# Feed-forward of a hybrid encoder layer: two plain hidden blocks ahead of the seven-product ones

## The chip, the cores and the metric

One core of a Trainium2 chip runs the whole program. Its engines are TensorE (PE, matrix products; PEld is its weight load), VectorE (DVE), ScalarE (ACT), GpSimd (POOL) and SyncE (SP, which here issues the DMAs). The metric is the device time of one execution in microseconds (us). Executions of one kernel agree to some tenths of a per cent.

## The reference

One inference step of a conditioned layer over 512 prompt tokens and 8 x 16 sample tokens, 640 in all, with a model width of 1024. Two attention branches, their merge and a gated residual come first; the change is in what follows them, the feed-forward part:

```python
h = modulate(rmsnorm(x, g_norm_ffn), shift2, scale2)
return x + gate2 * ((jax.nn.silu(h @ w_gate) * (h @ w_up)) @ w_down)
```

`w_gate` and `w_up` are 1024 x 2816 and `w_down` is 2816 x 1024. All data are 32-bit floats.

## The kernel before, in words

**Precision.** Every matrix operand is split in a high and a low part (`split`, L84 to L88: a cast on ACT, L86, and a subtraction on DVE, L87). Each product is three matmuls, high by high, high by low and low by high (`mm3`, L92 to L96).

**Blocks.** The 2816 hidden columns are 22 blocks of 128 (`fb` from 0 to 21). A block needs `silu(h @ w_gate)` and `h @ w_up` for its 128 columns and all 640 tokens. The tokens are cut into two halves of 320 (64 of each tile of 128), the 1024 rows of `h` into two halves of 512 (four groups of 128).

**Plain block.** Block 0 is computed directly (`plain`, L1258): 8 row groups by three matmuls for gate and for up, first for tokens 0 to 383 (384 columns a matmul), then for 384 to 639 (256 columns). That fills four PSUM banks of the tag `mm`. `first_block` (L1309) then makes silu, product and split, and after that a combination of quarters of `h`, the "fourth sum": for two halves of it, three DVE operations into a tile `t4` (L1323 to L1325), then a split that writes it over quarter 1 of `hB`, the operand that holds `h` in quarters (`hB[0]` high, `hB[1]` low parts). `t4` has the tag `sums`, of which there is one buffer.

**Seven products.** Blocks 1 to 21 (`ff_block`, L1336) treat gate and up, row halves and token halves as a 2 by 2 by 2 scheme with seven products of 12 matmuls (320 columns each) where eight would do. In program order: a11 (with `hB` 0, in a bank `pa`), s1 (with `hS` 0, in `pb`), the former block's last product (a22, with `hB` 1, which holds the fourth sum), the new a11 (with `hS` 1), s4 (with `hB` 3), a12 (with `hB` 2, in `pc`) and a21 (with `hS` 2). s1 and s4 are made by POOL from the loaded weights (L1342, L1345, L1346) in a tile of the tag `sums`, the same buffer that `t4` uses. `pa` is a bank of tag `mm`, `pb` and `pc` of tag `tr`; each tag has four banks.

**Loads.** Weights come through four buffers `w_raw` (`load_raw`, L172 to L179), two to a block (gate and up). Split operands lie in 12 buffers `op_hi` and 11 `op_lo`. After block 1 the gate rows of the residual are made (`gate_rows`), which load one row tile through the same buffers. After blocks 5, 10, 14, 18 and the last one, `down` multiplies the hidden columns so far by `w_down`.

**What stands ahead.** The output projection ends with tokens 512 to 639; `h2_stats` and `h2_cols` turn each tile of 128 tokens into columns of `hB` and, on POOL, into the differences that become `hS`. PE runs the gate and up products of block 0 for tokens 0 to 383, the transposes of the last token tile (`h2_cols(4)`, L140), then block 0 for tokens 384 to 639. The three splits of `hS` follow on ACT and DVE.

**Order.** The program is traced in source order; a planner orders each engine's queue by a simulated timeline before the program runs, and gives out buffers of a tag as they come free. On the chip each engine runs its queue in that fixed order and waits on semaphores for data and for buffers.

Of the kernel before, what the change touches and what calls it, by code (L numbers as in the profile page):

```python
# [34 lines left out]
NFF = FF // P  # L35
# [13 lines left out]
def layer_kernel(  # L49
# [10 lines left out]
    def nm(s):  # L60
        uid[0] += 1
        return f"{s}_{uid[0]}"
# [12 lines left out]
    def mm_tile():  # L75
        return psum.tile([P, 512], F32, tag="mm", bufs=4, name=nm("mm"))

    def tr_tile():
        return psum.tile([P, 512], F32, tag="tr", bufs=4, name=nm("tr"))

    def f(ap):
        return ap.bitcast(F32)

    def split(hi, lo, src, scale=None, eng=None):  # L84
        if scale is None:
            S.copy(hi, src)  # L86
            (eng or V).tensor_tensor(out=lo, in0=src, in1=f(hi), op=ALU.subtract)  # L87
        else:  # L88
            S.activation(out=hi, in_=src, func=AF.Copy, scale=scale)
            (eng or V).scalar_tensor_tensor(out=lo, in0=src, scalar=scale, in1=f(hi), op0=ALU.mult, op1=ALU.subtract)  # L90

    def mm3(out, lh, ll, rh, rl, start, stop, more=False):  # L92

        T.matmul(out, lh, rh, start=start, stop=False, skip_group_check=more)  # L94
        T.matmul(out, lh, rl, start=False, stop=False, skip_group_check=more)  # L95
        T.matmul(out, ll, rh, start=False, stop=stop, skip_group_check=more)  # L96
# [988 lines left out]
    def operand(src, n=512):  # L1085
        hi = wa.tile([P, 512], F32R, tag="op_hi", bufs=12, name=nm("ophi"))[:, :n]
        lo = wa.tile([P, 512], F32R, tag="op_lo", bufs=11, name=nm("oplo"))[:, :n]
        split(hi, lo, src)
        return hi, lo
# [18 lines left out]
    def gate_rows(c0, scale):  # L1108

        raw = ada_rows(c0)  # L1110
        parts = []
        for c in range(2):
            hi = wa.tile([P, 512], F32R, tag="op_hi", bufs=12, name=nm("ophi"))[0:AR, :]
            lo = wa.tile([P, 512], F32R, tag="op_lo", bufs=11, name=nm("oplo"))[0:AR, :]
            split(hi, lo, raw[:, c * 512:(c + 1) * 512])
            parts.append((hi, lo))
        out = []
        for v in range(2):
            g_ = gp.tile([P, DM], F32, tag=f"gate{v}", name=nm("gate"))
            for c in range(2):  # L1120
                cc = slice(c * 512, (c + 1) * 512)
                ps = mm_tile()
                T.matmul(ps, selr[:, v * P:(v + 1) * P], parts[c][0], start=True, stop=False)
                T.matmul(ps, selr[:, v * P:(v + 1) * P], parts[c][1], start=False, stop=True)
                S.activation(out=g_[:, cc], in_=ps, func=AF.Copy, scale=scale)
            out.append(g_)
        return out
# [103 lines left out]
    def ff_raw(fb):  # L1231
        cs_ = slice(fb * P, (fb + 1) * P)
        return [load_raw(v[:, :, cs_], [KD, P])[0] for v in (wg_v, wu_v)]
# [21 lines left out]
    def operands_of(fb):  # L1255
        return [[operand(r[:, i:i + 512]) for i in (0, 512)] for r in ff_raw(fb)]

    def plain(bank, w, t0, t1):  # L1258
        for k in range(KD):
            ks = slice(k % 4 * P, (k % 4 + 1) * P)  # L1260
            h = [x[:, k // 4 * 2:k // 4 * 2 + 2, k % 4, t0 * 64:t1 * 64] for x in hB]
            mm3(bank[:, :(t1 - t0) * P].rearrange("p (a x) -> p a x", a=2), w[k // 4][0][:, ks], w[k // 4][1][:, ks],
                h[0], h[1], k == 0, k == KD - 1)

    w0 = operands_of(0)
    banks0 = [mm_tile() for _ in range(4)]
# [16 lines left out]
    with pool("fwork") as fw:  # L1283
# [19 lines left out]
        def new_hidden():  # L1303
            for h, tag in ((aT, "aT"), (aTl, "aTl")):
                h.append(fw.tile([P, NT], F32R, tag=tag, bufs=6, name=nm(tag)))

        aT, aTl, tail = [], [], []

        def first_block():  # L1309
            new_hidden()  # L1310
            for i, (t0, t1) in enumerate(((0, 3), (3, 5))):
                n = (t1 - t0) * P
                u = fw.tile([P, 512], F32, tag="tmp", bufs=2, name=nm("u"))[:, :n]
                S.activation(out=u, in_=banks0[2 * i][:, :n], func=AF.Silu)
                V.tensor_tensor(out=u, in0=banks0[2 * i + 1][:, :n], in1=u, op=ALU.mult)
                o = [h[-1].rearrange("p (t a x) -> p a t x", a=2, x=64)[:, :, t0:t1, :] for h in (aT, aTl)]
                split(o[0], o[1], u.rearrange("p (a t x) -> p a t x", a=2, x=64))

            for k in range(0, 4, 2):
                k2 = slice(k, k + 2)  # L1320
                t4 = fw.tile([P, 2 * 512], F32, tag="sums", name=nm("t4"))[:, :2 * HALF]
                t4 = t4.rearrange("p (k x) -> p k x", k=2)
                V.tensor_tensor(out=t4, in0=f(hB[0][:, 2, k2]), in1=f(hS[0][:, 1, k2]), op=ALU.subtract)  # L1323
                V.tensor_tensor(out=t4, in0=t4, in1=f(hB[1][:, 2, k2]), op=ALU.add)
                V.tensor_tensor(out=t4, in0=t4, in1=f(hS[1][:, 1, k2]), op=ALU.subtract)  # L1325
                split(hB[0][:, 1, k2], hB[1][:, 1, k2], t4)
# [9 lines left out]
        def ff_block(fb):  # L1336

            new_hidden()
            a11, a12, a21, a22 = quarters(fb)
            sums = fw.tile([P, 2, 512], F32, tag="sums", name=nm("sums"))  # L1340
            s1, s4 = sums[:, 0], sums[:, 1]
            G.tensor_tensor(out=s1, in0=a21, in1=a22, op=ALU.add)  # L1342
            V.tensor_tensor(out=a21, in0=a11, in1=a21, op=ALU.subtract)
            o11 = operand(a11)
            G.tensor_tensor(out=a11, in0=s1, in1=a11, op=ALU.subtract)  # L1345
            G.tensor_tensor(out=s4, in0=a12, in1=a11, op=ALU.subtract)  # L1346
            pa, pb, pc = mm_tile(), tr_tile(), tr_tile()
            product(pa, o11, hB, 0)
            u1 = part(pa, "u1", 2)
            product(pb, operand(s1), hS, 0)  # L1350
            u5 = part(pb, "u5")
            last_product()
            product(pa, operand(a11), hS, 1, start=False)
            u2 = part(pa, "u2")
            product(pb, operand(s4), hB, 3, start=False)
            V.tensor_tensor(out=u2, in0=pb[:, :HALF], in1=u2, op=ALU.add)
            S.activation(out=u2, in_=u2, func=AF.Silu)
            product(pc, operand(a12), hB, 2)
            V.tensor_tensor(out=u1, in0=pc[:, :HALF], in1=u1, op=ALU.add)
            S.activation(out=u1, in_=u1, func=AF.Silu)  # L1360
            product(pa, operand(a21), hS, 2, start=False)
            u3 = part(pa, "u3")
            G.tensor_tensor(out=u3, in0=u3, in1=u5, op=ALU.add)
            G.tensor_tensor(out=u2, in0=u2, in1=u3, op=ALU.mult)
            hidden(1, u2)
            tail.append((pa, u1, a22, [h[-1].rearrange("p (t a x) -> p t a x", a=2, x=64)[:, :, 0, :]
                                       for h in (aT, aTl)]))

        def down(f0, f1):
            ks = range(f0, f1)  # L1370
            for c in range(2):
# [4 lines left out]
                for ts in ((0, 1), (2, 3), (4,)):  # L1376
# [5 lines left out]
                    for t in ts:  # L1382
# [3 lines left out]
                        if f1 == NFF:  # L1386
                            nc.sync.dma_start(y_flat[t][:, cc], x1[t][:, cc])

        first_block()
        ends = [0, 5, 10, 14, 18]  # L1390
        for fb in range(1, NFF):
            ff_block(fb)
            if fb == 1:
                gate2 = gate_rows(5 * DM, 1.0)
            if fb in ends:
                i = ends.index(fb)
                down(ends[i - 1], fb)
# [55 lines left out]
```

## Time and profile before

Three runs took 1180.89, 1182.13 and 1185.96 us. The profiled execution took 1190.14 us, and its span (first to last recorded instruction) is 1187.2 us.

| engine | busy us | share of the span | instructions |
|---|---|---|---|
| PE | 1122.8 | 95% | 7175 |
| DVE | 741.8 | 62% | 1680 |
| ACT | 564.0 | 48% | 1250 |
| POOL | 220.0 | 19% | 294 |

The feed-forward part begins at about 727 us of the span. A row of the timeline below gives the start, the time from the first start to the last end of the merged instructions, engine, source line, operation, output and inputs by the program's names, shape and count; in brackets stands the idle time of the engine before it and what ended that. PE's matmuls overlap in the records, so the distance from start to start is the pace, not the duration. `ophi` and `oplo` are the two parts of a split weight, `wraw` a loaded weight, `mm` and `tr` PSUM banks.

### The profile page before, as it was taken

What the parts mean: (1) busy time and instruction counts of PE and PEld (TensorE: products, weight loads), DVE (VectorE), ACT (ScalarE), POOL (GpSimd) and SP (SyncE); (2) the same over time, 40 slices, a digit from 0 to 9 for tenths busy, and PEclk for the clock granted to TensorE, in tenths of its full rate; (3) what the DMA queues carried; (4) which work ended last, traced back from release to release, by engine and by line L of the source; (5) the groups of instructions that cost most, each with busy time, mean ns of one, the idle gap of its engine ahead of it and who ended that gap; (6) DMA issues with size and microseconds to landing.
All of it is one profiled execution on the core that took longest, in us unless ns stands there. A gap on an engine that the chain in (4) does not pass through costs nothing.

```text
span 1187.2 us, 19414 instructions
## 1 busy us (share of the span) xinstructions
PE 1122.8 (95%) x7175; PEld 1005.6 (85%) x7175; DVE 741.8 (62%) x1680; ACT 564.0 (48%) x1250; POOL 220.0 (19%) x294
## 2 busy tenths in 40 slices
PE   7899999999899999899889998689999999999998
PEld 6669988999797788798788987689899899899896
DVE  3688565846675654455366357786586667676744
ACT  4675543445564554466543245465155236254340
POOL 0010001010000000112012214252243233342320
PEclk8999999999899999999999999799999999999999
DMA  8832344586565444766496220133123323123112
GB/s 267 301 96 76 111 148 135 167 240 192 170 181 152 137 153 146 236 213 228 122 296 211 84 68 18 36 107 109 52 71 107 89 65 113 37 90 106 54 55 88
DMA packets 156424, 158.15 MB, mean 133 GB/s; under 512 B 24826, under 2 KB 115495, under 8 KB 156330
## 3 DMA queue, kind: packets, MB, share of 16 engines
q1 hardware_dynamic: 156330, 156.92, 42.7%
q8 instruction: 56, 0.92, 0.3%
q14 instruction: 38, 0.31, 0.1%
HBM read 136.59 MB, written 20.30 MB: 132 GB/s over the span
## 4 chain that ended last, share of the span: by engine, by line
PE 80%; DMA 8%; DVE 5%; ACT 4%; issue 1%; SPq 1%; POOL 1%; ACTq 0%; POOLq 0%; DVEq 0%
PE mm L94 20%; PE mm L95 20%; PE mm L96 19%; PE tr L140 6%; PE tr L94 3%; PE tr L95 3%; PE tr L96 3%; DMA wraw<-in_w_in_dram 2%; DMA wraw<-in_w_o_a_dram 2%; PE mm L953 2%; PE mm L216 2%; DVE oplo L87 1%; DMA wraw<-in_w_up_dram 1%; DMA kn<-in_cache_band_k_dram 1%; PE mm L805 1%
## 5 line engine op out<-in xcount | busy, mean ns | idle before, releaser
L86 ACT CAST ophi<-wraw 128x512 fp32r<-128x512 f32 (+1 forms) x189 | 115.0, 622 | 134.5 <-PE mm L96 52.1
L87 DVE TENSOR_TENSOR oplo<-wraw,ophi 128x512 fp32r<-128x512 f32 (+1 forms) x189 | 147.9, 799 | 42.9 <-PE mm L96 17.2
L94 PE MATMUL mm<-ophi,aT 128*128 128x512 f32 x220 | 87.1, 396 | 0.4 <-DVE u L1333 0.3
L95 PE MATMUL mm<-oplo,aT 128*128 128x512 f32 x220 | 86.9, 395 | 0.0
L94 PE MATMUL mm<-hT_hi,whi 128*128 128x320 f32 x256 | 84.8, 331 | 1.7 <-ACT whi L86 1.3
L96 PE MATMUL mm<-ophi,aTl 128*128 128x512 f32 x220 | 86.1, 395 | 0.0
L96 PE MATMUL mm<-hT_hi,wlo 128*128 128x320 f32 x256 | 81.9, 320 | 0.0
L95 PE MATMUL mm<-hT_lo,whi 128*128 128x320 f32 x256 | 81.2, 317 | 0.0
L94 PE MATMUL mm<-whi,hT_hi 128*128 128x512 f32 (+3 forms) x240 | 79.4, 332 | 0.0
L96 PE MATMUL mm<-whi,hT_lo 128*128 128x512 f32 (+3 forms) x240 | 79.4, 332 | 0.0
L95 PE MATMUL mm<-wlo,hT_hi 128*128 128x512 f32 (+3 forms) x240 | 79.3, 331 | 0.0
L94 PE MATMUL mm<-hB,ophi 128*128 128x320 f32 (+2 forms) x200 | 62.9, 316 | 4.9 <-ACT hB L86 2.2
L95 PE MATMUL mm<-hB,ophi 128*128 128x320 f32 (+2 forms) x200 | 62.2, 312 | 0.6 <-DVE hB L87 0.6
L96 PE MATMUL mm<-hB,oplo 128*128 128x320 f32 (+2 forms) x200 | 62.1, 312 | 0.0
L1384 DVE TENSOR_TENSOR tmp<-mm,gate 128x512 f32<-128x512 f32 x50 | 34.3, 689 | 42.8 <-PE mm L96 42.7
L87 DVE TENSOR_TENSOR wlo<-wraw,whi 128x1024 fp32r<-128x1024 f32 (+2 forms) x36 | 41.0, 1141 | 30.1 <-ACT whi L86 29.4
L94 PE MATMUL mm<-hS,ophi 128*128 128x320 f32 x168 | 52.3, 311 | 3.7 <-ACT u L1293 3.7
L94 PEld LDWEIGHTS mm<-hT_hi,whi 128*128 128x128 f32 x256 | 50.3, 197 | 5.8 <-issue 2.1
L1342 POOL TENSOR_TENSOR sums<-wraw 128x512 f32<-128x512 f32 x21 | 30.2, 1437 | 129.7 <-DMA wraw<-in_w_up_dram 92.7
L86 ACT CAST ophi<-sums 128x512 fp32r<-128x512 f32 x42 | 26.1, 621 | 55.8 <-POOL sums L1342 19.1
L94 PE MATMUL tr<-hB,ophi 128*128 128x320 f32 x168 | 52.0, 309 | 0.0
L96 PE MATMUL mm<-hS,oplo 128*128 128x320 f32 x168 | 52.0, 309 | 0.0
(372 smaller groups left out, 3330.2 us busy)
## 6 DMA issues: line engine op xcount, KB each, us to landing
adaw<-in_w_ada_dram SPq DMA_DIRECT2D x48, 512.0 KB
wraw<-in_w_in_dram SPq DMA_DIRECT2D x28, 512.0 KB
wraw<-in_w_gate_dram SPq DMA_DIRECT2D x22, 512.0 KB
wraw<-in_w_up_dram SPq DMA_DIRECT2D x22, 512.0 KB
wraw<-in_w_down_dram SPq DMA_DIRECT2D x20, 512.0 KB
lat<-in_cache_kv_latent_dram SPq DMA_DIRECT2D x16, 512.0 KB
wraw<-in_cache_band_v_dram SPq DMA_DIRECT2D x16, 512.0 KB
kn<-in_cache_band_k_dram SPq DMA_DIRECT2D x16, 512.0 KB
```

The source lines that it names most:

```text
L86: S.copy(hi, src)
L87: (eng or V).tensor_tensor(out=lo, in0=src, in1=f(hi), op=ALU.subtract)
L94: T.matmul(out, lh, rh, start=start, stop=False, skip_group_check=more)
L95: T.matmul(out, lh, rl, start=False, stop=False, skip_group_check=more)
L96: T.matmul(out, ll, rh, start=False, stop=stop, skip_group_check=more)
L140: T.transpose(out, in_, ident[:k, :k])
L216: T.matmul(ps[q, :], cT[:, k, :], rvs[k // 2][:, k % 2, :], start=(k < 4), stop=(k >= 4))
L805: T.matmul(po[:, j * P:], both, st["PT"][1][:, c], start=False, stop=(j == 3))
L953: T.matmul(po[:, bs], st["lat"][:, j, bs] if j < 4 else lat_n[:, bs], st["PT"][:, j, :], start=(j == 0), stop=(j == 4))
L1342: G.tensor_tensor(out=s1, in0=a21, in1=a22, op=ALU.add)
L1384: V.tensor_tensor(out=tmp, in0=banks[t], in1=gate2[t // 4][:, cc], op=ALU.mult)
```

## The change

The function `first_block` is cut in two: `plain_block(banks0)`, which does silu, product and split for any four banks, and `fourth_sum`, which does the rest. Block 1 becomes a plain block like block 0, in the four banks of the tag `tr`; its weights are loaded and split as block 0's are (`operands_of(1)`). The fourth sum stands behind both plain blocks in the source. The seven-product blocks start with block 2, and the gate rows are made after block 2 instead of block 1. `plain`, `operands_of`, `ff_block` and `down` are unchanged.

```diff
-        def first_block():
+        def plain_block(banks0):
             new_hidden()
             for i, (t0, t1) in enumerate(((0, 3), (3, 5))):
...
                 split(o[0], o[1], u.rearrange("p (a t x) -> p a t x", a=2, x=64))
+
+        def fourth_sum():
 
             for k in range(0, 4, 2):
...
-        first_block()
+        plain_block(banks0)
+        w1 = operands_of(1)
+        banks1 = [tr_tile() for _ in range(4)]
+        for i, (t0, t1) in enumerate(((0, 3), (3, 5))):
+            for j in range(2):
+                plain(banks1[2 * i + j], w1[j], t0, t1)
+        plain_block(banks1)
+        fourth_sum()
         ends = [0, 5, 10, 14, 18]
-        for fb in range(1, NFF):
+        for fb in range(2, NFF):
             ff_block(fb)
-            if fb == 1:
+            if fb == 2:
                 gate2 = gate_rows(5 * DM, 1.0)
```

## Rows read from the trace of the kernel before

**Rows 1.** Page, part 4: the chain that ended last, by engine.
```profile
PE 80%; DMA 8%; DVE 5%; ACT 4%; issue 1%; SPq 1%; POOL 1%; ACTq 0%; POOLq 0%; DVEq 0%
```

**Rows 2.** Windows of 20 us: length, busy time (instructions) by engine, granted clock, DMA.
```profile
780.00:800.00 20.00, 17.25 (x112) 16.20 (x112) 17.81 (x21) 10.96 (x23) 11.74 (x10) 1.00 0.35 105
...
880.00:900.00 20.00, 20.00 (x138) 20.00 (x137) 14.51 (x22) 10.60 (x24) 8.66 (x8) 1.00 0.30 87
```

**Rows 3.** Timeline of PE from 734 to 772 us.
```profile
734.85 0.34 PE L94 MATMUL mm<-hB,ophi 128*128 128x384 f32 x1
...
736.76 0.34 PE L96 MATMUL mm<-hB,oplo 128*128 128x384 f32 x1
...
740.21 0.51 PE L94 MATMUL mm<-hB,ophi 128*128 128x256 f32 x2 [2.25 <-ACT hB L86]
741.31 0.39 PE L95 MATMUL mm<-hB,ophi 128*128 128x256 f32 x1 [0.59 <-DVE hB L87]
...
744.97 0.28 PE L96 MATMUL mm<-hB,oplo 128*128 128x256 f32 x1
...
746.74 0.28 PE L96 MATMUL mm<-hB,oplo 128*128 128x256 f32 x1
749.07 0.42 PE L94 MATMUL mm<-hB,ophi 128*128 128x320 f32 x1 [2.05 <-ACT u L1314]
...
760.20 0.63 PE L94 MATMUL tr<-hS,ophi 128*128 128x320 f32 x1 [8.34 <-ACT ophi L86]
...
763.74 0.32 PE L94 MATMUL mm<-hS,ophi 128*128 128x320 f32 x1
...
767.30 0.85 PE L1123 MATMUL mm<-ophi,selr 106*128 106x512 f32 x3
...
770.20 0.31 PE L94 MATMUL mm<-hS,ophi 128*128 128x320 f32 x1
...
771.81 0.31 PE L96 MATMUL mm<-hS,oplo 128*128 128x320 f32 x1
```

**Rows 4.** Windows of a few us around the same place, columns as in rows 2.
```profile
741.30:747.00 5.70, 5.69 (x46) 5.51 (x46) 5.70 (x4) 3.03 (x3) 1.71 (x2) 1.00 0.01 3
...
750.00:752.00 2.00, 1.86 (x8) 1.46 (x6) 2.00 (x5) 0.67 (x3) 0.00 (x0) 0.51 0.00 0
...
762.00:763.70 1.70, 1.70 (x8) 1.70 (x7) 1.00 (x1) 0.93 (x2) 1.29 (x2) 0.50 0.00 0
```

**Rows 5.** Timeline of ACT.
```profile
739.54 1.23 ACT L86 CAST hB<-hfull 128x512 fp32r<-128x512 f32 x2 [5.77 <-DVE hfull L1220]
...
752.22 0.73 ACT L86 CAST hB<-t 128x640 fp32r<-128x640 f32 x1
756.41 0.73 ACT L86 CAST hB<-t 128x640 fp32r<-128x640 f32 x1 [3.47 <-DVE t L1325]
759.53 0.62 ACT L86 CAST ophi<-sums 128x512 fp32r<-128x512 f32 x1 [2.38 <-POOL sums L1342]
...
763.93 2.71 ACT L86 CAST ophi<-wraw 128x512 fp32r<-128x512 f32 x5
```

**Rows 6.** Timeline of DVE.
```profile
737.62 1.29 DVE L1219 TENSOR_TENSOR hfull<-tr,A 128x512 f32<-128x512 f32 x2 [3.10 <-PE tr L140]
...
750.26 0.42 DVE L1315 TENSOR_TENSOR u<-mm,u 128x256 f32<-128x256 f32 x1
...
752.98 0.82 DVE L87 TENSOR_TENSOR hB<-t,hB 128x640 fp32r<-128x640 f32 x1 [0.77 <-ACT hB L86]
753.84 0.82 DVE L1323 TENSOR_TENSOR t<-hB,hS 128x640 f32<-128x640 f32 x1
```

**Rows 7.** Timeline of POOL.
```profile
758.23 1.26 POOL L1342 TENSOR_TENSOR sums<-wraw 128x512 f32<-128x512 f32 x1 [15.22 <-DVE hB L87]
```

**Rows 8.** Timeline of SP: a gate load; the chain in order of time: an up load.
```profile
718.93 0.39 SPq L178 DMA_DIRECT2D wraw<-in_w_gate_dram  x1
...
765.41 3.81 DMA wraw<-in_w_up_dram
```

## The prediction

> **What bounds the kernel now.** I read the chain of waits first: PE carries 80% of it, so only what PE does, or waits for, moves the time [rows 1]. Then the windows: from about 802 us on PE has no opening (a 20 us window holds 20.00 us of matmul), while 780 to 800 holds 17.25 [rows 2]. Then PE's timeline at the place of the change, looking for idle times in brackets [rows 3]. The reader is to see four openings there. Two, 2.25 and 0.59 us, stand before block 0's matmuls for tokens 384 to 639, which wait for the last columns of `hB`. One of 2.05 us stands before block 1's first product, which wants an `mm` bank while all four hold block 0. The longest, 8.34 us (751.86 to 760.20), stands before s1 and ends with the cast of s1's weights.
>
> Why s1 is so late is read backwards over the other engines. The cast (759.53) waited for POOL's sum [rows 5]; POOL had idled 15.22 us and was released by a split of `hB` on DVE [rows 7]. That split belongs to the fourth sum: its tile `t4` and s1 share the single `sums` buffer. So this is a serial chain: cast of the first half (752.22), its low part (752.98), three sums of the second half (the first at 753.84), cast (756.41), low part, POOL, cast, PE at 760.20 [rows 3, 5, 6, 7]. From the first cast to PE's start it takes 760.20 - 752.22 = 7.98 us.
>
> The clock adds to it. At 741 to 747 it is granted at 1.00, at 750 to 752 at 0.51 and at 762 to 763.7 at 0.50 [rows 4], the lower of its two levels. At full level 12 matmuls of 320 columns follow each other at (771.81 - 770.20)/11 = 0.146 us, 1.76 us for 12. The 12 of a11 from 749.07 took 2.79 us (to 751.86), the 12 of s1 3.54 us (760.20 to 763.74) [rows 3]: 1.03 + 1.78 = 2.8 us lost. With the openings of 2.05 and 8.34 the start of the seven-product blocks loses 13.2 us.
>
> **The change part by part.**
>
> *Matmuls.* Block 1 loses 7 x 12 = 84 matmuls of 320 columns, 84 x 0.146 = 12.3 us. It gains 48 of 384 and 48 of 256 columns. Their pace is (736.76 - 734.85)/11 = 0.174 and (746.74 - 744.97)/15 = 0.118 us [rows 3], so 8.3 + 5.7 = 14.0 us. Cost: +1.7 us.
>
> *The bank wait.* The new block writes `tr` banks; the last transposes left them when DVE read them, from 737.62 on [rows 6], well before 747. The 2.05 us go. What is next late there is nothing: `hB` is complete and block 0 ran at full clock up to that point.
>
> *The openings before it.* Two of the `tr` banks are free even before the last transposes, and block 1's tokens 0 to 383 need none of the late columns, so matmuls of block 1 can run in the 2.25 + 0.59 = 2.84 us openings at 738 to 741.3. The planner does put ready PE work ahead of the source order: gate-row matmuls stand at 767.30 between products [rows 3]. They need block 1's split weights by then: three casts and three low parts more than before. ACT idles 5.77 us up to 739.54 and DVE 3.10 us up to 737.62 [rows 5, 6]; three casts of about 0.54 (2.71/5, rows 5) take 1.6. Between all 2.84 us and none I take all, since the cover is there.
>
> *The extra splits* can also fall in front of the token statistics, which PE waits for at that time. Nothing bounds this below zero (earlier operands make nothing earlier here); above, all three pairs in front give 3 x 2 x 0.62 = 3.7. I take one cast, 0.6.
>
> *The fourth sum* moves behind the new block, and gets a new wait. Its splits write quarter 1 of `hB`; block 1 as a plain block still reads that quarter, in the first half of each bank's 24 matmuls, last in the fourth bank. Full-clock PE would go 747.0 + 14.0 - 2.84 = 758.2 for the end of block 1; the fourth bank starts 24 x 0.118 = 2.8 earlier, at 755.4, and row groups 0 and 1 (6 matmuls) are read by 756.1. Only then may the cast of 752.22 run. The chain behind it is the same 7.98 us, because `sums` still has one buffer, plus two DVE operations of 0.42 of block 1's second half that now fall into it [rows 6]: 8.8 us. s1 reaches PE at 756.1 + 0.1 + 8.8 = 765.0. PE has meanwhile done block 1 and a11 of block 2 (1.76): it is free at 760.0. So an opening of 5.0 us stays, in the old place and for the old reason. Behind the waiting cast on ACT stand the silu of the last banks and s1's cast; for both PE waits only through this chain.
>
> Could PE fill it? a12 needs no sum, its weights were loaded long before, and ACT idled 3.47 and 2.38 us inside the old opening; yet a12's cast stood in the five at 763.93, behind s4's [rows 5]. Operand buffers go out in source order. I count no filling.
>
> *After s1* the rest runs as from 760.20 on before, with the clock at its lower level for s1: 1.78. If it stays at full level up to 1 us is won, since the new a11 is not split sooner.
>
> The row shows 0.50 behind an opening of 8.34 us and 1.00 behind 2.84 [rows 4]; 5.0 lies between. The Trainium skill, "TensorE: Matmul & The Clock Gate", section "HAM oscillation — how this bites in real kernels", says that a long enough idle stretch brings the lower clock back, so it too puts s1 at the lower level; kept warm, the sum would be up to 1 us less.
>
> *Loads and gate rows.* The row tile of the gate now stands behind block 2's two loads in SP's queue. Buffers go out in order, so block 2's gate load takes the row tile's former place, its up load takes that of 718.93 instead of 765.41 [rows 8], and the row tile comes when block 1's casts free a buffer. Block 3's up load then waits for a12 of block 2, just as block 2's at 765.41 waited for block 1. So blocks 3 to 5 should repeat blocks 2 to 4, openings included (20.00 - 17.25 = 2.75 us of them in 780 to 800, rows 2): nothing, between 2.75 less and 2.75 more.
>
> **The sum.** Lost before: 13.2. Lost after: 1.7 (matmuls) + 5.0 (opening) + 1.8 (clock) - 2.84 (filled) + 0.6 (casts) = 6.3. Gain 6.9 us. The profiled execution of 1190.14 would be 1183.2. It lies 8.0 above the median of the runs shown; the same 6.9 from 1182.13 give **1175.2 us**. Its own range, with the clock, the casts and half of the later blocks' bound: 1172.5 to 1178.
>
> **The rivals.**
>
> *The early openings stay empty* (the splits come too late, or the planner sees no opening). Then block 1 ends at 761.0, s1 starts 2.84 later: gain 4.1, 1178.0. For it: DVE is 2.00 of 2.00 busy at places [rows 4]. Against it: the idle times above.
>
> *The whole start closes up.* If POOL's sum gets the `sums` buffer ahead of the fourth sum's second half, or other products fill PE, nothing waits: 13.2 - 1.7 + 2.84 - 0.6 = 13.7 gained, 1168.4. For it: the fourth sum is wanted only by the last product of block 2. Against it: buffers of a tag went out in source order in every case seen. The Trainium skill, "Perfetto Trace Analysis", section "Matmul Optimizations", asks for all eight PSUM banks to be used, and by that rule alone this is what happens; the trace's longest opening, however, is not one of banks.
>
> *Blocks 3 to 5 starve (slower).* One load takes 3.81 us from issue to landing [rows 8]. If the new order of loads makes each of three blocks wait a whole load, POOL's sum of 1.26 and the cast of 0.62 [rows 5, 7], that is 3 x 5.7 = 17.1 against some 4.5 now: 12.6 lost, 6.9 won, 1187.8. It decides from 2.3 us more per block on. For it: 780 to 800 is where DVE and POOL are busiest [rows 2]. Against it: the buffers free up at the same points of the cycle.
>
> *The casts get in the way* of the token statistics fully, and nothing is filled: gain 1.0, 1181.
>
> **How the numbers follow.** Forecast 0.48, empty openings 0.25, closes up 0.10, starving 0.10, casts 0.07. No change means within 0.5% (5.9 us), about what a measurement of this kernel can tell: 1176.2 to 1188.0. Faster by more: 0.72 of the forecast (0.35), 0.2 of the second case (0.05) and the third (0.10), 0.50. Slower by more: part of the starving case and what no case covers, 0.10. The rest 0.40. The range for 8 in 10 reaches from inside the third case to the weak end of the fourth: 1169 to 1183.5.
>
> **What would show it.** Right: no idle before the first matmul of a `tr` bank from `hB`; matmuls of block 1 at 738 to 741; an opening of about 5 us before the first `tr` from `hS`, ended by a cast of `sums`, with a cast of `hB` from `t` released by PE shortly before the end of block 1. Wrong: no such opening, PE reading a12's product inside it, or new openings of over 2 us each in blocks 3 to 5.

## The result and the profile after

The changed kernel takes 1170.9 us (median of four runs, 1170.75 to 1172.05). The kernel before takes 1184.05 us (four runs, 1180.89 to 1186.29; three of them are the runs that the forecast starts from, with 1182.13 as their median). The ratio is 0.9901, with a 95% interval of 0.9873 to 0.9929: faster by some 12 us by the ratio and 13 by the medians, where 6.9 us of gain were forecast. 1175.2 us was predicted.

The profiled executions took 1190.14 us before and 1172.05 us after, with spans of 1187.2 and 1170.3 us. Those 16.9 us are not all the work of the change. PE runs the same 4631 recorded matmuls in the same order up to the end of the output projection, yet that point lies at 723.89 us of the span before and at 714.72 us after. Of these 9.2 us, 9.1 are there already where the projection starts. Before:
```profile
666.56 0.39 PE L94 MATMUL mm<-ophi,mT 128*128 128x512 f32 x1
```
After:
```profile
657.43 0.39 PE L94 MATMUL mm<-ophi,mT 128*128 128x512 f32 x1
```
The first instruction of any engine that the edit adds or moves comes later: a load of weights, issued at 685.51 us of the changed kernel. So the 9 us are lost or won ahead of anything that was edited. From the end of the projection to the end it is 463.3 us before and 455.6 us after: 7.7 us. I call this stretch the rest, and use it as the measure of the change. Windows of the rest in the two kernels, with the columns of [rows 2]:

The kernel before:
```profile
723.89:1187.20 463.31, 438.28 (x2544) 403.34 (x2544) 310.58 (x461) 198.14 (x393) 144.36 (x114) 0.98 0.25 76
```
The changed kernel:
```profile
714.72:1170.30 455.58, 437.59 (x2556) 404.37 (x2556) 305.36 (x459) 193.25 (x383) 138.45 (x109) 0.99 0.25 77
```
PE has 12 matmuls more and nearly the same busy time; what shrinks is the time in which PE does nothing, from 25.0 to 18.0 us (463.31 - 438.28 and 455.58 - 437.59), and the granted clock is a little higher.

The totals of the changed kernel, part 1 of its page, to be set beside the table of before:
```profile
PE 1113.9 (95%) x7187; PEld 998.9 (85%) x7187; DVE 737.1 (63%) x1675; ACT 560.3 (48%) x1243; POOL 214.1 (18%) x289
```

The timeline of PE in the changed kernel, with the columns of [rows 3]:
```profile
719.36 0.69 PE L94 MATMUL mm<-hB,ophi 128*128 128x384 f32 x1 [4.64 <-ACT hB L86]
720.86 0.69 PE L95 MATMUL mm<-hB,ophi 128*128 128x384 f32 x1 [0.50 <-DVE hB L87]
...
732.36 0.34 PE L94 MATMUL tr<-hB,ophi 128*128 128x384 f32 x1
...
737.39 0.40 PE L94 MATMUL mm<-hB,ophi 128*128 128x256 f32 x2
...
746.38 0.28 PE L94 MATMUL tr<-hB,ophi 128*128 128x256 f32 x1
...
752.06 0.31 PE L94 MATMUL mm<-hB,ophi 128*128 128x320 f32 x1
...
758.52 0.63 PE L94 MATMUL tr<-hS,ophi 128*128 128x320 f32 x1 [4.54 <-ACT ophi L86]
...
762.03 0.31 PE L94 MATMUL mm<-hS,ophi 128*128 128x320 f32 x1
...
785.21 0.41 PE L94 MATMUL mm<-hS,ophi 128*128 128x320 f32 x1 [1.26 <-ACT u L1293]
...
790.71 0.41 PE L94 MATMUL mm<-hS,ophi 128*128 128x320 f32 x1 [2.02 <-ACT u L1293]
```
Of the four openings of [rows 3] three are gone. Matmuls of block 1 (`tr<-hB`, 384 columns) run from 732.36 on, and the 256-column matmuls of block 0 at 737.39 follow without a bracket, where 2.25 and 0.59 us stood. The wait for a bank, 2.05 us, has no successor. Before s1 4.54 us stay of 8.34. New are the first two lines: 4.64 and 0.50 us of opening right behind the projection, where the kernel before had one of 2.18 us:
```profile
726.07 1.28 PE L140 MATMUL tr<-ident,xn 128*128 128x128 f32 x5 [2.18 <-ACT xn L1195]
```
The order of PE has changed there too. Before, the transposes of the fourth token tile come first; after, block 0's matmuls do, and the transposes follow at 726.43.

The same places on ACT, the changed kernel:
```profile
710.50 1.67 ACT L86 CAST ophi<-wraw 128x512 fp32r<-128x512 f32 x3
...
712.69 1.13 ACT L86 CAST ophi<-wraw 128x512 fp32r<-128x512 f32 x2
...
715.07 0.29 ACT L107 ACTIVATE rst<-ss,eps 128x1 f32<-128x1 f32 x1 [1.24 <-DVE ss L1192]
...
718.70 1.12 ACT L86 CAST hB<-hfull 128x512 fp32r<-128x512 f32 x2
...
750.13 0.73 ACT L86 CAST hB<-t 128x640 fp32r<-128x640 f32 x1 [0.26 <-PE tr L96]
...
754.74 0.72 ACT L86 CAST hB<-t 128x640 fp32r<-128x640 f32 x1 [0.30 <-DVE t L1327]
757.85 0.62 ACT L86 CAST ophi<-sums 128x512 fp32r<-128x512 f32 x1 [2.38 <-POOL sums L1344]
```
The first four lines are the new opening. Five casts of weights go out ahead of the statistics of the fourth of the five token tiles (715.07), and ahead of the columns of the third (718.70), which PE's first matmul of block 0 waits for. Four of the five belong to block 1; one stands there in the kernel before as well (719.67). The last three are the predicted chain of the fourth sum: a cast over `hB` that a matmul of block 1 releases (750.13), the second half (754.74), the cast of s1's weights (757.85); [rows 5] has the same three at 752.22, 756.41 and 759.53, the first of them without a wait for PE.

And on POOL, to [rows 7]:
```profile
756.56 1.26 POOL L1344 TENSOR_TENSOR sums<-wraw 128x512 f32<-128x512 f32 x1 [19.01 <-DVE hB L87]
```
POOL still idles until a split of `hB` on DVE gives it the one buffer `sums`.

Last, windows of the changed kernel, columns as before:
```profile
714.70:719.40 4.70, 0.06 (x2) 0.05 (x1) 4.70 (x14) 2.66 (x7) 0.92 (x1) 0.81 0.70 193
719.40:722.00 2.60, 2.10 (x6) 1.59 (x7) 2.57 (x5) 2.08 (x4) 2.00 (x3) 0.50 0.08 22
722.00:724.00 2.00, 2.00 (x8) 2.00 (x8) 0.81 (x6) 1.13 (x2) 0.00 (x0) 0.50 0.00 0
...
736.00:747.00 11.00, 11.00 (x82) 11.00 (x82) 9.46 (x11) 6.34 (x9) 1.55 (x2) 1.00 0.01 2
...
758.50:760.00 1.50, 1.48 (x5) 1.25 (x6) 0.69 (x2) 0.00 (x0) 1.38 (x1) 0.51 0.00 0
```
In the first, PE does nothing while DVE is busy for all of it (4.70 of 4.70 us); the five subtractions that go with the casts run from 713.08 to 716.55, ahead of the third tile's columns and between them. Behind each of the two openings the granted clock is at 0.50 or 0.51, the lower of the two levels; over the filled stretch from 736 to 747 it is 1.00, and PE has no gap.

### The profile page after: what moved, and what is told of

Its sections match the earlier page's. It is cut to its first block, busy times and chain, and to the rows that moved or that the text cites. A ratio compares the mean times of both kernels' runs of the same rounds, so it can differ in the third digit from the quotient of the medians.

```text
span 1170.3 us, 19416 instructions
## 1 busy us (share of the span) xinstructions
PE 1113.9 (95%) x7187; PEld 998.9 (85%) x7187; DVE 737.1 (63%) x1675; ACT 560.3 (48%) x1243; POOL 214.1 (18%) x289
## 5 line engine op out<-in xcount | busy, mean ns | idle before, releaser
L94 PE MATMUL mm<-hB,ophi 128*128 128x320 f32 (+2 forms) x192 | 60.2, 316 | 4.6 <-ACT hB L86 4.6
L95 PE MATMUL mm<-hB,ophi 128*128 128x320 f32 (+2 forms) x192 | 60.1, 314 | 0.5 <-DVE hB L87 0.5
L94 PE MATMUL tr<-hB,ophi 128*128 128x320 f32 (+2 forms) x192 | 59.2, 309 | 0.0
L95 PE MATMUL tr<-hB,ophi 128*128 128x320 f32 (+2 forms) x192 | 59.2, 309 | 0.0
L96 PE MATMUL tr<-hB,oplo 128*128 128x320 f32 (+2 forms) x192 | 58.6, 309 | 0.0
L94 PE MATMUL mm<-hS,ophi 128*128 128x320 f32 x160 | 49.6, 310 | 3.3 <-ACT u L1293 3.3
```

## The experiments

Three questions were left: how much of the 16.9 us belongs to the change, what the new opening behind the projection costs and why it came, and what the fourth sum and the banks are worth. In the texts below, as here, the measure is the rest, read from the profile of each run; the changed kernel profiled a second time gave 455.8 us, 0.2 from the first. The other rests come from one profile each, and the granted clock can differ from one profile to the next behind the same opening (last section). The interval stands behind the ratio to the kernel before, run on the same chip in the same round.

| kernel | end of projection | span | rest | against after | median us (runs) | ratio to before (95%) |
|---|---|---|---|---|---|---|
| before | 723.89 | 1187.2 | 463.3 | +7.7 | | |
| after | 714.72 | 1170.3 | 455.6 | | 1170.9 (4) | 0.9901 (0.9873 to 0.9929) |
| again | 715.29 | 1171.1 | 455.8 | +0.2 | 1175.07 (12) | 0.9943 (0.9917 to 0.9969) |
| before_late_sum | 714.60 | 1172.4 | 457.8 | +2.2 | 1175.68 (12) | 0.9949 (0.9928 to 0.9970) |
| after_late_sum | 716.00 | 1165.4 | 449.4 | -6.2 | 1167.93 (6) | 0.9889 (0.9858 to 0.9921) |
| after_pool_lows | 714.46 | 1171.1 | 456.6 | +1.0 | 1173.85 (12) | 0.9945 (0.9923 to 0.9967) |
| after_mm_banks | 715.14 | 1176.9 | 461.8 | +6.2 | 1179.36 (12) | 0.9986 (0.9967 to 1.0005) |
| after_shared_weights | 719.55 | 1171.8 | 452.3 | -3.3 | 1171.71 (6) | 0.9908 (0.9881 to 0.9935) |
| after_casts_behind | 722.20 | 1173.4 | 451.2 | -4.4 | 1170.26 (6) | 0.9916 (0.9889 to 0.9942) |
| both_edits | 712.93 | 1157.2 | 444.3 | -11.3 | 1162.31 (6) | 0.9835 (0.9808 to 0.9862) |

The runs of before had medians of 1181.2 us beside again to after_pool_lows and 1182.65 us beside the other four.

**again.** No edit: the changed kernel a second time, with more runs.

> The changed kernel once more, nothing altered, to part the change from what happens ahead of it. In the two profiles the feed-forward stage (from the opening before the last token tiles' transposes or block 0 on, 723.89 before and 714.72 after) is 7.7 us shorter, and 9.2 us are already gone before it, in a part whose instruction order is the same in both. Theory A (the 9.2 us are a state of single executions of the kernel before): the time ratio to the kernel before comes nearer to 0.9935 (7.7 us) than 0.990, or the runs of the kernel before lie in two groups some 5 us apart, and 100 to 400 us of the span look like one of the two profiles at hand. Rival B (the change itself makes the earlier part shorter): ratio 0.988 to 0.990 again, all runs near 1171, and the same start of the feed-forward stage, 714 to 715 us.

The ratio came out at 0.9943, 6.7 us of 1181.2, nearer to the 6.9 forecast than to the first reading. Single runs of one kernel spread over 1174.68 to 1188.58 us (before, in one band and not in two groups) and 1169.36 to 1180.87 us (after). That is some one per cent, more than the tenths of a per cent that the first three runs showed, and the 1190.14 us of the profile of before lie above all of them. So the first comparison had its share of luck: the 7.7 us of the rest would be a ratio of 0.9935 (1 - 7.7/1184), inside the second interval and just outside the first. Where the scatter sits can be seen ahead of the change, in one window of the two profiles. The kernel before:
```profile
310.00:320.00 10.00, 8.75 (x41) 8.37 (x42) 7.05 (x23) 5.34 (x16) 0.00 (x0) 0.67 0.21 52
```
The changed kernel, the same stage:
```profile
310.00:320.00 10.00, 10.00 (x72) 9.72 (x71) 8.69 (x25) 6.62 (x17) 1.29 (x1) 1.00 0.54 168
```
The same program has a granted clock of 0.67 in the one execution and of 1.00 in the other; in before an opening of 3.45 us at 307.80 goes ahead of it, in after one of 1.50 us.

**after_casts_behind.** Block 1's splits are ordered behind the scaling of the last token tile (its rows are multiplied by what the statistics give):
```diff
+        xn_last[0] = S.activation(out=xn, in_=x1[t], func=AF.Copy, scale=rs)
...
-        w1 = operands_of(1)
+        with tc.issue_after(xn_last[0].ins):
+            w1 = operands_of(1)
```

> The changed kernel with the casts of block 1's weights queued on ACT behind the scaling of the last token tile (L1195), so that none can stand ahead of the statistics. Theory A (place of the splits): the first opening is about 2.2 us again, block 1's matmuls still fill the opening at the 256-column matmuls, 2 to 3.5 us faster than the changed kernel. Rival B (ACT's casts harmless, DVE or PE's new order make the opening): the opening stays over 4 us; or the splits now come too late and PE waits for them before block 1: no gain.

The rest fell by 4.4 us, where 2 to 3.5 were expected. PE's timeline in this kernel, whose projection ends at 722.20:
```profile
723.04 1.09 PE L140 MATMUL tr<-ident,xn 128*128 128x128 f32 x8 [0.84 <-ACT xn L1196]
...
725.18 0.44 PE L94 MATMUL mm<-hB,ophi 128*128 128x384 f32 x1 [1.05 <-ACT hB L86]
```
and ACT's:
```profile
730.02 1.15 ACT L1196 ACTIVATE xn<-x,rs 128x1024 f32<-128x1024 f32 x1
731.08 2.69 ACT L86 CAST ophi<-wraw 128x512 fp32r<-128x512 f32 x5
```
The five casts now stand behind the last scaling, the openings are 0.84 and 1.05 us instead of 4.64 and 0.50, and the transposes of a token tile that the changed kernel had pushed to 726.43 are first again. So the place of the splits is the cause of the new opening. The granted clock of 722.2 to 727 is 1.00, against 0.50 at the same place of the changed kernel. That slow stretch can't be put down to the new opening alone, since the kernel before has 0.52 behind its 2.18 us too (last section). 4.4 is therefore more than the cost of block 1's splits: the edit also moves the split that before had there, and takes away part of an opening (0.84 + 1.05 for 2.18) and a slow stretch that before had as well. By whole runs the effect can't be told: 0.9916 against 0.9901 and 0.9943.

**after_shared_weights.** Block 1 uses block 0's split weights; its own four splits and two loads are left out, so that this kernel is for measuring alone:
```diff
-        w1 = operands_of(1)
+        w1 = w0
```

> The changed kernel in which block 1 takes block 0's split weights: the load and the four splits of block 1's own weights are left out. Theory A (these splits, the casts on ACT as much as the subtractions on DVE, come ahead of the statistics of the last token tiles): without them the transposes of token tile 3 stand again right behind the output projection, the first opening falls from 4.6 to about 2.2 us and 2 to 3.5 us are gained over the changed kernel. Rival B (the planner's order there changes because a fifth to eighth bank is wanted, not because of the splits): the opening stays over 4 us.

3.3 us less, inside the 2 to 3.5 that were expected. The first opening behind the projection (719.55) is about that of before again:
```profile
721.75 0.33 PE L140 MATMUL tr<-ident,xn 128*128 128x128 f32 x1 [2.19 <-ACT xn L1195]
```
This is the price of having block 1's splits at that time: 3.3 us, of which the longer opening is 2.95 (5.14 against 2.19).

**after_pool_lows.** The four subtractions of block 1's weights go to POOL, the casts stay:
```diff
-        w1 = operands_of(1)
+        w1 = [[operand(r[:, i:i + 512], eng=G) for i in (0, 512)] for r in ff_raw(1)]
```

> The changed kernel with the low parts of block 1's four weight splits made by POOL instead of DVE. Theory A (the opening of 4.64 us before block 0, against 2.18 before the change, comes from these subtractions on DVE ahead of the token statistics): it falls back to 2 to 3 us and the low clock behind it shortens, 2 to 4 us faster than the changed kernel. Rival B (the casts on ACT or the planner's new order of the statistics make it): the opening stays at 4 us or more and the time within 1 us; POOL's subtractions (1.3 us each by its other rows) may also delay the token differences and so cost up to 3 us.

No gain, 1.0 us worse in the rest. PE's openings are 3.57 and 2.02 us, in sum 5.59 where they were 5.14:
```profile
718.03 0.45 PE L94 MATMUL mm<-hB,ophi 128*128 128x384 f32 x1 [3.57 <-ACT hB L86]
...
720.67 0.69 PE L95 MATMUL mm<-hB,ophi 128*128 128x384 f32 x1 [2.02 <-DVE hB L87]
```
and on POOL and DVE
```profile
712.31 5.86 POOL L87 TENSOR_TENSOR oplo<-wraw,ophi 128x512 fp32r<-128x512 f32 x4
...
712.82 1.24 DVE L1192 TENSOR_TENSOR ss<-sq 128x1 f32<-128x1 f32 x1
```
POOL takes 5.86/4 = 1.47 us for one where DVE takes 0.68, and its own work for the differences of the tokens comes after. DVE, which was to be relieved, ran slower beside it: the sum above takes 1.24 us where the changed kernel has 0.15 (at 714.89), and DVE's one remaining subtraction takes 1.31 (at 714.51). Three of its small instructions end within 0.02 us of the end of one of POOL's: 714.06, 716.96 and 718.18, with POOL's ends at 714.04, 716.94 and 718.17. So this run doesn't tell whether PE waited for DVE's time or for the order of the splits; it took work from DVE and slowed DVE at once. The two runs above tell that it was the splits at this place.

**after_mm_banks.** Block 1 takes the banks of block 0's tag:
```diff
-        banks1 = [tr_tile() for _ in range(4)]
+        banks1 = [mm_tile() for _ in range(4)]
```

> The changed kernel with the second plain block in the four mm banks of the first instead of the four tr banks. Theory A (the other banks remove the bank wait and let block 1 run in the opening before block 0's last tokens): block 1's matmuls begin only when silu has read a bank, an opening of about 2 us comes back before them and the 2.2 to 2.8 us before the 256-column matmuls too; with the fourth sum's chain that much later, 4 to 6 us slower than the changed kernel. Rival B (the banks don't matter, only the fourth sum's place does): within 1.5 us of the changed kernel.

6.2 us more, just over the 4 to 6 that were expected: without the other banks the change gains 1.5 us of its 7.7 in the rest, and the ratio's interval holds 1. The openings before the 256-column matmuls are back:
```profile
735.06 0.80 PE L94 MATMUL mm<-hB,ophi 128*128 128x256 f32 x2 [2.22 <-ACT hB L86]
736.14 0.58 PE L95 MATMUL mm<-hB,ophi 128*128 128x256 f32 x1 [0.29 <-DVE hB L87]
```
but the wait for a bank, which I had expected as a second opening of 2 us, did not come. The windows say why:
```profile
738.00:740.00 2.00, 2.00 (x12) 2.00 (x11) 2.00 (x2) 1.16 (x2) 0.00 (x0) 0.50 0.00 0
...
744.30:760.00 15.70, 15.70 (x109) 15.53 (x107) 6.93 (x14) 3.45 (x7) 0.00 (x0) 1.00 0.00 1
```
Behind the opening the clock is granted at 0.50, and the 48 matmuls of 256 columns take 9.11 us from the first start to the next matmul (735.06 to 744.17, with the 0.29 us of idle) instead of 5.68. By then the bank is free, and PE runs on without a gap. The bank was free no earlier than when silu had read it, at 743.84:
```profile
743.35 0.49 ACT L1314 ACTIVATE u<-mm 128x384 f32<-128x384 f32 x1
```
At the pace of full clock the 48 would have ended at about 741.0 (735.06 + 5.68 + 0.29), and PE would have waited some 2.8 us for the bank: an estimate from these rows. So the slow clock filled the time of the bank's wait and hardly added to it, and by this estimate the price of doing without the banks is about the same at either clock. In whole runs it is 0.9986 against 0.9943, some 5 us.

**before_late_sum.** The kernel before, with the fourth sum alone moved behind block 1:
```diff
+        def fourth_sum():
...
             if fb == 1:
+                fourth_sum()
                 gate2 = gate_rows(5 * DM, 1.0)
```

> The kernel before with one edit alone: the fourth sum is traced behind block 1's products (it is wanted only by block 1's last product), no second plain block. Theory A (the 8.34 us opening is the shared sums buffer): POOL's s1 of block 1 starts as soon as hS is split (about 747 on the old time axis), the 8.34 us opening and the low clock behind it (2.8 us) go, the 2.05 us bank wait stays: about 10 us faster than before, as much as the change brought in its own stage or more. Rival B (the opening has another cause, such as the load of the weights or the rebuilt pools): the opening stays above 6 us and the time within 3 us of before.

5.5 us gained, about half of what I expected. Of the opening before s1 a wait of 1.34 us for s1's low part is left, and half of its length comes back one block later:
```profile
740.11 0.42 PE L94 MATMUL mm<-hB,ophi 128*128 128x320 f32 x1 [0.92 <-ACT u L1314]
743.78 0.42 PE L96 MATMUL tr<-hS,oplo 128*128 128x320 f32 x1 [1.34 <-DVE oplo L87]
...
761.40 0.41 PE L94 MATMUL tr<-hS,ophi 128*128 128x320 f32 x1 [3.99 <-ACT ophi L86]
```
because on POOL the sum of block 2 now waits for the buffer:
```profile
738.33 1.28 POOL L1344 TENSOR_TENSOR sums<-wraw 128x512 f32<-128x512 f32 x1 [4.29 <-PE mm L96]
...
759.43 1.26 POOL L1344 TENSOR_TENSOR sums<-wraw 128x512 f32<-128x512 f32 x1 [2.71 <-DVE hB L87]
```
The buffer `sums` is handed on in source order, and here the sum that comes behind the fourth sum waits for it.

**after_late_sum.** The same move in the changed kernel, behind the first seven-product block:
```diff
         plain_block(banks1)
-        fourth_sum()
...
             if fb == 2:
+                fourth_sum()
                 gate2 = gate_rows(5 * DM, 1.0)
```

> The changed kernel with the fourth sum traced behind block 2's products. Theory A (the 4.54 us opening before the first product of hS is the write-after-read wait on hB's quarter 1 plus the shared sums buffer): the opening falls under 1 us, the low clock behind it (1.9 us) goes too, 5 to 6.5 us faster than the changed kernel. Rival B (the opening is s1's own work on POOL and ACT, or its load): it stays above 3 us and the time within 1.5 us of the changed kernel.

6.2 us gained, as expected. PE's timeline:
```profile
755.34 0.31 PE L96 MATMUL mm<-hB,oplo 128*128 128x320 f32 x1
755.48 0.31 PE L94 MATMUL tr<-hS,ophi 128*128 128x320 f32 x1
...
767.89 0.31 PE L94 MATMUL tr<-hS,ophi 128*128 128x320 f32 x1
```
and POOL's:
```profile
763.74 1.30 POOL L1344 TENSOR_TENSOR sums<-wraw 128x512 f32<-128x512 f32 x1 [13.93 <-DVE hB L87]
```
s1 follows a11 without a gap, at full clock (its 12 matmuls go from 755.48 to 757.24, 1.76 us). The opening of 4.54 us and the 1.75 us that the low clock cost s1 make 6.29. Here the buffer comes back in time: POOL makes block 3's sum at 763.74, once the fourth sum's split has released the buffer, and PE takes it up at 767.89 without idling. Same move, same buffer; that it is the plain block 1 which gives the chain time is my reading, and no run tests it.

**both_edits.** The last two gains together, the fourth sum late and block 1's splits behind the scaling.

> Fourth sum behind block 2's products and block 1's casts behind the last token tile's scaling, in one kernel. If the two causes are apart, their gains add: 6 to 6.5 us and 2 to 3.5 us, together 8 to 10 us faster than the changed kernel, about 1162 to 1164 where the changed kernel has 1172. If what one frees only uncovers the other's wait, no more than 7 us.

The rest is 444.3 us, 11.3 below the changed kernel; 6.2 and 4.4 make 10.6, and 8 to 10 were expected, so the two causes add, and neither edit uncovers the other's wait. In whole runs it is 1162.31 us (1158.73 to 1165.16), ratio 0.9835, the fastest version of the study: its interval lies wholly below those of the changed kernel (both comparisons), and its median is 5.6 us below that of after_late_sum, the next, whose interval it just touches (0.9858 and 0.9862). PE's timeline, projection ending at 712.93:
```profile
713.77 1.09 PE L140 MATMUL tr<-ident,xn 128*128 128x128 f32 x8 [0.84 <-ACT xn L1196]
...
715.91 0.68 PE L94 MATMUL mm<-hB,ophi 128*128 128x384 f32 x1 [1.05 <-ACT hB L86]
...
748.34 0.31 PE L94 MATMUL tr<-hS,ophi 128*128 128x320 f32 x1
```

## Why the prediction was right, and where it was not

The time lay 4.3 us below the forecast: inside the range for 8 in 10 (1169 to 1183.5), and 1.6 us under the forecast's own (1172.5 to 1178). The gain in the stage of the change was 7.7 us against 6.9, yet that nearness is luck in part, since it hides two misses that cancel.

| step | predicted us | measured us |
|---|---|---|
| matmuls, cost | 1.7 | 1.7, as far as read: the 48 of 256 columns took 752.06 - 746.38 = 5.68, forecast 5.66 |
| bank wait, gone | 2.05 | 2.05: no idle before any `tr<-hB` |
| early openings, filled | 2.84 | 2.84: 29 matmuls of block 1 run there, no idle |
| opening before s1, stays | 5.0 | 4.54 (753.98 to 758.52) |
| clock in s1, lost | 1.8 | 1.75: 12 matmuls took 3.51 |
| casts in the way, cost | 0.6 | 3.3 (splits left out) |
| later blocks | 0 (±2.75) | 2.9 gained |

With the measured terms the sum is 13.2 - (1.7 + 4.54 + 1.75 - 2.84 + 3.3) + 2.9 = 7.65, the 7.7 us of the rest.

*The opening before s1* stayed for the reason that was named: quarter 1 of `hB` is overwritten only when block 1 has read it, and `sums` has one buffer. From the cast at 750.13 to PE at 758.52 it is 8.39 us, forecast 8.8. after_late_sum shows the cause, since the opening goes when the fourth sum goes. Which of the two, the overwriting or the one buffer, would hold s1 by itself was not tried.

*The banks* did what the forecast said: with them, block 1 fills the openings that before had at 738 to 741 (here just ahead of 737.39). after_mm_banks shows that this is most of the change's gain, 6.2 of 7.7 us, where the forecast had 2.05 + 2.84 = 4.9 on it. Of the 6.2, 5.7 lie ahead of s1: from the end of the projection to s1 it is 49.49 us there (715.14 to 764.63) and 43.80 in the changed kernel (714.72 to 758.52).

*The casts* are the term that was sized wrong: "I take one cast, 0.6", between 0 and 3.7. No row stood behind the choice within these bounds. The forecast saw idle time for the splits on ACT and DVE ahead of the last tile's columns; the planner put block 1's splits at 710.5 to 716.6 instead, ahead of the fourth token tile's statistics and the third's columns. (Their loads had been issued at 683.10 and 684.31.) The openings behind the projection grew from 2.18 to 5.14 us in two pieces, and a token tile's transposes fell behind block 0's matmuls. The measured 3.3 lies inside the bounds, near the upper one: all of block 1's pairs stood in front, and not one cast. The rival "the casts get in the way fully" had this mechanism right, though it coupled it with openings that stay empty, and these were filled.

*The later blocks* were costed at nothing, as a shifted repetition. From s1 to the first product of `down` it was 66.68 us before (760.20 to 826.88) and 51.50 after (758.52 to 810.02). Block 1's 84 matmuls are 12.3 of the difference; 2.9 us are left. The openings in this stretch sum up to 4.53 us before and to 3.28 after (1.26 and 2.02, the last two lines of the timeline above), and the matmuls between them follow each other more closely. So 1.25 us of the 2.9 are openings, and the rest is pace. This is outside the ±2.75 by a hair. What in the loads' order gave it was not tried: whether the gate rows' load behind block 2, or POOL's work at other times, stays open. From the start of `down` on both kernels take 360.3 us.

*The 4.3 us* between forecast and median are within the scatter ahead of the change, where one and the same point moves by 11 us between profiles; the twelve runs of again have their median at 1175.07.

The two cases that the prediction set against itself did not come. Nothing starved in blocks 3 to 5: one opening there, of 2.02 us, is over the 2 us that were named as a sign, and not one in each block. And the start did not close up: PE filled nothing of the 4.54 us. The Trainium skill, "Perfetto Trace Analysis", section "Matmul Optimizations", asks for all eight PSUM banks to be used; after_mm_banks, which has four of them for the two plain blocks, agrees with it, at 6.2 us, and the 4.54 us that stayed with all eight in use are the part that banks don't reach.

## What to carry to other kernels

Work that can be done early is not free where a planner puts it in front: look at what stands behind it on its engine, and give it an order behind the chain that PE waits for (3.3 to 4.4 us here). Moving it to another engine is no way out by itself (1.0 us worse on POOL, with DVE slowed beside it). A second set of PSUM banks pays where it lets PE work ahead into an opening. An opening's price is its length and, where the clock is lower behind it, that too: 4.54 and 1.75 us before s1. A slow stretch that ends in a wait costs little more than the wait: in after_mm_banks it filled the time until the bank was free. When a long buffer chain is moved, ask who is next to want the same buffer: the same move brought 5.5 of some 10 us in one kernel and all 6.2 in the other.

## What was not expected of the hardware

One order of 4631 matmuls reached the same point, the end of the projection, between 712.93 and 723.89 us in the ten profiles (712.93 and 722.20 in two of the same round), with the granted clock differing from one execution to the next in stages that no edit touched. A difference of one per cent between two spans is then read stage by stage.

The lower clock also followed short openings, and not each time. Behind 2.18 us before the transposes at 726.07 the kernel before shows
```profile
726.00:729.40 3.40, 3.33 (x14) 3.33 (x15) 2.86 (x6) 2.36 (x7) 2.96 (x3) 0.52 0.00 0
```
and after_mm_banks has 0.50 behind 2.22 and 0.29 us, while the kernel before has 1.00 behind 2.25 and 0.59 us [rows 3, 4]. Even 0.84 and 1.05 us can be followed by either level: after_casts_behind has 1.00 behind them, and both_edits, with the same two openings, has
```profile
716.00:719.30 3.30, 3.30 (x10) 3.06 (x11) 3.20 (x8) 2.08 (x7) 2.31 (x3) 0.50 0.00 0
```
so that both_edits is 1.3 us longer from the end of the projection to the first 256-column matmul (18.29 and 17.03 us). What decides between these was not settled.
